# Relu and row sums: partition 4g+i reads row block g+32i, and the first row's sums are stored as 128 words

## The chip, the core and the metric

The kernel runs on one core of a Trainium2 chip. The metric is device time in microseconds (us), the median over several runs. The profiled execution is one run with the hardware profiler on. Engines named here: ACT (ScalarE), DVE (VectorE), SP (SyncE, which only issues DMAs in this kernel) and 16 DMA engines, which serve SP's one queue of transfers.

## The reference

```python
batch, seq, dim = 32, 512, 1024
x = np.random.randn(batch, seq, dim).astype(np.float32)

def reference(x):
    relu_x = np.maximum(x, 0)
    return np.sum(relu_x, axis=-1).astype(np.float32)
```

There are 16384 rows of 1024 float32 numbers (4 KB each, 67.1 MB together). Each row gives one number: the sum of its positive elements.

## The kernel before

**Rows and partitions.** SBUF has 128 partitions, so each partition gets 128 rows. The rows of DRAM are cut in three regions one after another, `REGIONS = [1, 111, 16]`: the first 128 x 1 rows, the next 128 x 111, the last 128 x 16. Within a region partition p takes block p, a contiguous piece of 1, 111 or 16 rows (lines 45 to 48, `xv`). `ov` (line 49) is the same cut of the output. `res` holds a partition's 128 sums, one column for each of its rows.

**Loads.** `buf` has three slots (`NB = 3`) of 16 rows each. Seven chunks of 16 rows (`CHUNKS`) go through the slots in turn; the first chunk is one row of the region of 1 and 15 rows of the region of 111, in two DMAs. These first two issues are moved ahead of the drain in the program's preamble (line 96), so that they are the first thing that SP does. Line 91 issues the chunks. From the fourth on, SP waits first until DVE has finished with the slot (`s_dve`, line 87). Lines 101, 112 and 115 issue the tail, the region of 16 rows: pieces of 8, 4 and 2 rows (`TAIL`), then two rows cut in four parts, the last of which lands in a tile of its own, `seam`. Behind these, still on SP, stand three stores: the sums of the first row (L117), those of the region of 111 rows (L123), and those of the tail (L207).

**Arithmetic.** For the first six chunks ACT applies the relu in place to several rows in one instruction (L145), and DVE sums the rows (L160), in the steps that `ACT_STEPS` and `DVE_STEPS` list; a few rows are done by one instruction each that does relu and sum at once, on ACT (L127) or DVE (L130). The last chunk and the tail are done in this second way, alternating between the engines. The two last rows are put together from parts in `seam`, and the last two sums release L207.

**The first row's sums.** Column 0 of `res` holds the sums of the first 128 rows of x, one in each partition. DVE transposes `res[:, 0:32]` in blocks of 32 x 32 into `turned` once the second chunk is done (L169), so that four partitions hold 32 consecutive sums each. SP waits for that (`s_turn`) and stores them as 4 pieces of 128 bytes (L117).

Of the kernel before, what the change touches and what calls it, by code (L numbers as in the profile page):

```python
# [3 lines left out]
P = 128  # L4
D = 1024
BIG = 16
NB = 3
REGIONS = [1, 111, 16]
# [3 lines left out]
TAIL = [8, 4, 2]  # L12
CUT = 912
HEAD = 256


def bass_relu_sum_kernel(
    nc: bass.Bass,
    x: bass.AP,
    out: bass.AP,  # L20
):

    fp32 = mybir.dt.float32
    ALU = mybir.AluOpType
    AF = mybir.ActivationFunctionType
    X = mybir.AxisListType.X

    B, S, _ = x.shape
    J = B * S // P
    NBIG = len(CHUNKS)
    assert BIG * NBIG + sum(TAIL) + 2 == J == sum(REGIONS)  # L40

    xr = x.rearrange("b s d -> (b s) d")
    of = out.rearrange("b s -> (b s)")
    start = [sum(REGIONS[:i]) for i in range(len(REGIONS))]
    xv = [
        xr[P * s : P * (s + n), :].rearrange("(p j) d -> p j d", p=P)
        for s, n in zip(start, REGIONS)
    ]
    ov = [of[P * s : P * (s + n)].rearrange("(p j) -> p j", p=P) for s, n in zip(start, REGIONS)]

    buf = nc.alloc_sbuf_tensor("buf", [P, NB, BIG, D], fp32)
    w = D - CUT
    seam = nc.alloc_sbuf_tensor("seam", [P, 2 + w + HEAD + 2], fp32)
    res = nc.alloc_sbuf_tensor("res", [P, J], fp32)
    turned = nc.alloc_sbuf_tensor("turned", [P, 32], fp32)

    n_in = NBIG + len(TAIL) + 3
    s_in = [nc.alloc_semaphore(f"s_in{i}") for i in range(n_in)]
    s_act = nc.alloc_semaphore("s_act")
    s_dve = nc.alloc_semaphore("s_dve")  # L60
    s_fact = nc.alloc_semaphore("s_fact")
    s_fdve = nc.alloc_semaphore("s_fdve")
    s_half = nc.alloc_semaphore("s_half")
    s_seam = nc.alloc_semaphore("s_seam")
    s_last = nc.alloc_semaphore("s_last")
    s_turn = nc.alloc_semaphore("s_turn")
    s_store = nc.alloc_semaphore("s_store")
    s_out = nc.alloc_semaphore("s_out")

    sp, act, dve = nc.sync, nc.scalar, nc.vector  # L70

    NTWO = len(ACT_STEPS)
    done = [sum(map(len, DVE_STEPS[: c + 1])) for c in range(NTWO)]


    tb = NBIG % NB


    code = nc.main_func.blocks[0].instructions
    arrival = next(  # L80
        i
        for i, ins in enumerate(code)
        if ins.engine == mybir.EngineType.SP and type(ins).__name__ == "InstDrain"
    )
    for c in range(NBIG + 1):
        if c >= NB:
            sp.wait_ge(s_dve, done[c - NB])
        if c < NBIG:
            i = 0
            for g, j, n in CHUNKS[c]:  # L90
                sp.dma_start(  # L91
                    out=buf[:, c % NB, i : i + n, :], in_=xv[g][:, j : j + n, :]
                ).then_inc(s_in[c], 16)
                i += n
                if c == 0:
                    code.insert(arrival, code.pop())
                    arrival += 1
    r = 0
    tail = []
    for i, n in enumerate(TAIL):  # L100
        sp.dma_start(out=buf[:, tb, r : r + n, :], in_=xv[-1][:, r : r + n, :]).then_inc(  # L101
            s_in[NBIG + i], 16
        )
        tail.append((r, n, s_in[NBIG + i]))
        r += n


    rows = xv[-1].rearrange("p j d -> p (j d)")[:, r * D : (r + 2) * D]
    flat = buf[:, tb, r : r + 2, :].rearrange("p j d -> p (j d)")
    first, second, third = [(0, CUT), (D + D // 2, 2 * D), (D + HEAD, D + D // 2)]  # L110
    for k, (lo, hi) in enumerate((first, second, third)):
        sp.dma_start(out=flat[:, lo:hi], in_=rows[:, lo:hi]).then_inc(  # L112
            s_in[NBIG + len(TAIL) + k], 16
        )
    sp.dma_start(out=seam[:, 2 : 2 + w + HEAD], in_=rows[:, CUT : D + HEAD]).then_inc(s_seam, 16)
    sp.wait_ge(s_turn, 1)
    sp.dma_start(  # L117
        out=of[0:P].rearrange("(k q) -> k q", q=32), in_=turned[0:P:32, 0:32]
    ).then_inc(s_store, 16)
    sp.wait_ge(s_fact, 1)  # L120
    sp.wait_ge(s_fdve, 1)
    sp.wait_ge(s_in[-1], 16)
    sp.dma_start(out=ov[1][:, :], in_=res[:, start[1] : start[2]]).then_inc(s_store, 16)  # L123


    def on_act(t, acc):
        return act.activation(t, t, AF.Relu, accum_out=acc)  # L127

    def on_dve(t, acc):
        return dve.tensor_scalar(  # L130
            out=t, in0=t, scalar1=0.0, scalar2=None, op0=ALU.max, op1=ALU.add, accum_out=acc
        )

    def row(c, i):
        return buf[:, c % NB, i, :], res[:, c * BIG + i : c * BIG + i + 1]

    k = 0
    for c in range(NTWO):
        alone = BIG - sum(ACT_STEPS[c])
        act.wait_ge(s_in[c], 16 * len(CHUNKS[c]))  # L140
        r = 0
        ready = []
        for n in ACT_STEPS[c]:
            t = buf[:, c % NB, r : r + n, :]
            act.activation(t, t, AF.Relu).then_inc(s_act, 1)  # L145
            k += 1
            ready += [k] * n
            r += n
        for i in range(BIG - alone // 2, BIG):
            on_act(*row(c, i))  # L150
        if alone:
            dve.wait_ge(s_in[c], 16 * len(CHUNKS[c]))
            for i in range(BIG - alone, BIG - alone // 2):
                on_dve(*row(c, i))
        r = seen = 0
        for n in DVE_STEPS[c]:
            if ready[r + n - 1] > seen:
                seen = ready[r + n - 1]
                dve.wait_ge(s_act, seen)
            dve.tensor_reduce(  # L160
                out=res[:, c * BIG + r : c * BIG + r + n],
                in_=buf[:, c % NB, r : r + n, :],
                axis=X,
                op=ALU.add,
            ).then_inc(s_dve, 1)
            r += n
        if c == 1:
            dve.wait_ge(s_dve, done[c])
            dve.transpose(out=turned[:, :], in_=res[:, 0:32]).then_inc(s_turn, 1)  # L169


    j0 = NBIG * BIG
    for c in range(NTWO, NBIG):
        act.wait_ge(s_in[c], 16 * len(CHUNKS[c]))
        dve.wait_ge(s_in[c], 16 * len(CHUNKS[c]))
        for i in range(BIG):
            ins = (on_act if i % 2 else on_dve)(*row(c, i))
            if i >= BIG - 2:
                ins.then_inc(s_fact if i % 2 else s_fdve, 1)
    for r, n, s in tail:  # L180
        act.wait_ge(s, 16)
        dve.wait_ge(s, 16)
        for i in range(r, r + n):
            f = on_act if (i - r) % 2 else on_dve
            f(buf[:, tb, i, :], res[:, j0 + i : j0 + i + 1])

    lo, hi = first
    act.wait_ge(s_in[-3], 16)
    dve.wait_ge(s_in[-3], 16)
    on_act(flat[:, lo : CUT // 2], seam[:, 0:1]).then_inc(s_half, 1)  # L190
    on_dve(flat[:, CUT // 2 : hi], seam[:, 1:2]).then_inc(s_half, 1)
    k = 2 + w
    lo, hi = second
    act.wait_ge(s_in[-2], 16)
    on_act(flat[:, lo:hi], seam[:, k + HEAD : k + HEAD + 1]).then_inc(s_seam, 1)
    lo, hi = third
    dve.wait_ge(s_in[-1], 16)
    on_dve(flat[:, lo:hi], seam[:, k + HEAD + 1 : k + HEAD + 2]).then_inc(s_seam, 1)
    act.wait_ge(s_seam, 16 + 2)
    act.wait_ge(s_half, 2)  # L200
    on_act(seam[:, 0:k], res[:, J - 2 : J - 1]).then_inc(s_last, 1)
    dve.wait_ge(s_seam, 16 + 2)
    on_dve(seam[:, k : k + HEAD + 2], res[:, J - 1 : J]).then_inc(s_last, 1)


    sp.wait_ge(s_last, 2)
    sp.dma_start(out=ov[-1][:, :], in_=res[:, start[-1] : J]).then_inc(s_out, 16)  # L207
    sp.wait_ge(s_store, 16 * (len(REGIONS) - 1))
    sp.wait_ge(s_out, 16)


# [26 lines left out]
```

## Time and profile before

| | |
|---|---|
| median of 3 runs | 160.86 us (160.80 to 160.87) |
| span of the profiled execution | 159.4 us |
| what lies around the span (160.86 less 159.39) | 1.47 us |
| DVE busy | 120.6 us, 59 instructions |
| ACT busy | 101.5 us, 54 instructions |
| DMA packets | 2457, 67.18 MB, 421 GB/s over the span |

The profiled execution has no time of its own beside its span, which runs from the first to the last instruction of the program; the median of the runs stands for the whole. Times in views are in us from the start of the span. Besides the views of the profile, three records of the trace are used: the time and size of each DMA packet, the start and length of each DMA issue on SP, and the times at which the 16 engines add to a DMA's semaphore. Their figures for the kernel before:

| bytes of a packet | count | shortest ns | mean ns | longest ns |
|---|---|---|---|---|
| 4096 (first row) | 128 | 159 | 198 | 620 |
| 61440 (15 rows) | 128 | 2267 | 2289 | 2547 |
| 65536 (16 rows) | 768 | 2418 | 2421 | 2513 |
| 32768 (tail, 8 rows) | 128 | 1213 | 1213 | 1213 |
| 444 (L123's store) | 128 | 22 | 24 | 29 |
| 128 (L117's store) | 4 | 13 | 13 | 13 |
| 64 (L207's store) | 128 | 8 | 10 | 11 |
| 4 (semaphore writes) | 276 | 7 | 9 | 14 |

### The profile page before, as it was taken

To read this page: it belongs to the slowest core of one execution; us is meant where nothing else is said; L and a number is where in the kernel's file an instruction comes from. 1 tells how busy PE (TensorE), PEld (TensorE's weight loads), DVE (VectorE), ACT (ScalarE), POOL (GpSimd) and SP (SyncE) were. 2 spreads that over 40 slices of the span, in tenths; PEclk is the share of its full clock that TensorE was granted. 3 is DMA by queue.
4 is the path that set the end of the run, shared out by engine and by line. 5 is a ranking of instruction groups with operands and counts; after the bars stand their busy time and mean duration, and the time that the engine had idled before them with its cause. 6 is when DMAs were issued, how large, how long until landed. Compare 5 with 4: busy or idle time off the path is not lost.

```text
span 159.4 us, 150 instructions
## 1 busy us (share of the span) xinstructions
DVE 120.6 (76%) x59; ACT 101.5 (64%) x54; POOL 0.2 (0%) x4
## 2 busy tenths in 40 slices
DVE  0000000009999999999999999999999999898995
ACT  3000059980799708996099941999329980496975
POOL 0000000000000000000000000000000000000000
DMA  9997996996996997989979969969969979798994
GB/s 378 493 401 339 493 526 263 526 526 263 526 493 296 526 444 345 526 378 411 526 312 477 526 263 526 526 263 526 526 263 526 444 345 526 321 469 374 417 400 142
DMA packets 2457, 67.18 MB, mean 421 GB/s; under 512 B 536, under 2 KB 792, under 8 KB 1176
## 3 DMA queue, kind: packets, MB, share of 16 engines
q1 hardware_dynamic: 2456, 67.18, 98.1%
q14 instruction: 1, 0.01, 0.0%
HBM read 67.11 MB, written 0.07 MB: 421 GB/s over the span
## 4 chain that ended last, share of the span: by engine, by line
DVE 55%; DMA 34%; ACT 9%; SPq 2%; issue 0%
DVE res L160 54%; DMA buf<-in_x_dram 34%; ACT buf L145 9%; SPq L101 1%; SPq L112 1%; DVE buf L130 0%; DVE seam L130 0%; SPq L91 0%; DVE turned L169 0%
## 5 line engine op out<-in xcount | busy, mean ns | idle before, releaser
L160 DVE TENSOR_REDUCE res<-buf 128x4 f32<-128x4096 f32 (+3 forms) x18 | 99.4, 5596 | 35.5 <-ACT buf L145 35.5
L145 ACT ACTIVATE buf<-buf 128x7168 f32<-128x7168 f32 (+5 forms) x13 | 80.4, 6233 | 46.1 <-DMA buf<-in_x_dram 46.1
L127 ACT ACTIVATE buf<-buf 128x1024 f32<-128x1024 f32 (+2 forms) x19 | 19.0, 999 | 8.9 <-DMA buf<-in_x_dram 8.9
L130 DVE TENSOR_SCALAR_CACHE_REDUCE buf<-buf 128x1024 f32<-128x1024 f32 (+2 forms) x19 | 20.7, 1143 | 1.7 <-DMA buf<-in_x_dram 1.6
L127 ACT ACTIVATION_READ_ACCUMULATOR buf<-buf 128x1 f32 x19 | 3.6, 188 | 0.0
L145 ACT ACT_TABLE_LOAD x1 | 1.3, 1283 | 1.3 <-PEq L223 1.3
L130 DVE DVE_READ_ACCUMULATOR buf<-buf 128x1 f32 x19 | 1.6, 84 | 0.0
L130 DVE TENSOR_SCALAR_CACHE_REDUCE seam<-seam 128x258 f32<-128x258 f32 x1 | 0.4, 421 | 0.0
L127 ACT ACTIVATE seam<-seam 128x114 f32<-128x114 f32 x1 | 0.3, 300 | 0.1
L169 DVE STREAM_TRANSPOSE turned<-res 128x32 f32<-128x32 f32 x1 | 0.2, 211 | 0.0
L127 ACT ACTIVATION_READ_ACCUMULATOR seam<-seam 128x1 f32 x1 | 0.2, 186 | 0.0
L223 POOL MEMSET const-bfloat16-1.0<- 128x1 bf16 x1 | 0.1, 101 | 0.0
L223 POOL MEMSET const-uint8-127<- 128x1 uint8 x1 | 0.1, 101 | 0.0
L223 POOL MEMSET const-float32-0.0<- 128x1 f32 x1 | 0.1, 98 | 0.2 <-issue 0.2
L223 POOL MEMSET const-float32-1.0<- 128x1 f32 x1 | 0.1, 98 | 0.0
L130 DVE DVE_READ_ACCUMULATOR seam<-seam 128x1 f32 x1 | 0.1, 82 | 0.0
## 6 DMA issues: line engine op xcount, KB each, us to landing
buf<-in_x_dram SPq DMA_DIRECT2D x1, 7680.0 KB, 21.1
buf<-in_x_dram SPq DMA_DIRECT2D x1, 4096.0 KB, 25.3
buf<-in_x_dram SPq DMA_DIRECT2D x1, 2048.0 KB, 29.9
buf<-in_x_dram SPq DMA_DIRECT2D x1, 1024.0 KB, 31.9
buf<-in_x_dram SPq DMA_DIRECT2D x1, 512.0 KB, 3.3
buf<-in_x_dram SPq DMA_DIRECT2D x1, 456.0 KB, 32.5
buf<-in_x_dram SPq DMA_DIRECT2D x1, 256.0 KB, 32.7
seam<-in_x_dram SPq DMA_DIRECT2D x1, 184.0 KB, 32.6
```

The lines of the kernel that those rows point to most:

```text
L101: sp.dma_start(out=buf[:, tb, r : r + n, :], in_=xv[-1][:, r : r + n, :]).then_inc(s_in[NBIG + i], 16)
L112: sp.dma_start(out=flat[:, lo:hi], in_=rows[:, lo:hi]).then_inc(s_in[NBIG + len(TAIL) + k], 16)
L127: return act.activation(t, t, AF.Relu, accum_out=acc)
L130: return dve.tensor_scalar(out=t, in0=t, scalar1=0.0, scalar2=None, op0=ALU.max, op1=ALU.add, accum_out=acc)
L145: act.activation(t, t, AF.Relu).then_inc(s_act, 1)
L160: dve.tensor_reduce(out=res[:, c * BIG + r : c * BIG + r + n], in_=buf[:, c % NB, r : r + n, :], axis=X, op=ALU.add,).then_inc(s_dve, 1)
L169: dve.transpose(out=turned[:, :], in_=res[:, 0:32]).then_inc(s_turn, 1)
L223: nc = _bacc.Bacc("TRN2", target_bir_lowering=False, num_devices=1)
```

## The change

In each region partition 4g+i (g from 0 to 31, i from 0 to 3) takes block g+32i in the place of block 4g+i. The pieces stay contiguous and of the same size. On the DRAM side the access pattern of each load and store becomes one of 32 x 4 pieces; on the SBUF side it stays one of 128 partitions. The first row's sums are stored from column 0 of `res` directly, as 128 words of 4 bytes, once the first chunk is summed; the transpose, `turned` and `s_turn` go. `last` is 0 and `j0` is 112, so the pieces of the tail and the columns of `res` stay as they were.

```diff
--- before.py
+++ after.py
@@ -43,16 +43,18 @@
     of = out.rearrange("b s -> (b s)")
     start = [sum(REGIONS[:i]) for i in range(len(REGIONS))]
     xv = [
-        xr[P * s : P * (s + n), :].rearrange("(p j) d -> p j d", p=P)
+        xr[P * s : P * (s + n), :].rearrange("(i g j) d -> g i (j d)", i=4, g=P // 4)
         for s, n in zip(start, REGIONS)
     ]
-    ov = [of[P * s : P * (s + n)].rearrange("(p j) -> p j", p=P) for s, n in zip(start, REGIONS)]
+    ov = [
+        of[P * s : P * (s + n)].rearrange("(i g j) -> g i j", i=4, g=P // 4)
+        for s, n in zip(start, REGIONS)
+    ]
 
     buf = nc.alloc_sbuf_tensor("buf", [P, NB, BIG, D], fp32)
     w = D - CUT
     seam = nc.alloc_sbuf_tensor("seam", [P, 2 + w + HEAD + 2], fp32)
     res = nc.alloc_sbuf_tensor("res", [P, J], fp32)
-    turned = nc.alloc_sbuf_tensor("turned", [P, 32], fp32)
 
     n_in = NBIG + len(TAIL) + 3
     s_in = [nc.alloc_semaphore(f"s_in{i}") for i in range(n_in)]
@@ -63,7 +65,6 @@
     s_half = nc.alloc_semaphore("s_half")
     s_seam = nc.alloc_semaphore("s_seam")
     s_last = nc.alloc_semaphore("s_last")
-    s_turn = nc.alloc_semaphore("s_turn")
     s_store = nc.alloc_semaphore("s_store")
     s_out = nc.alloc_semaphore("s_out")
 
@@ -74,6 +75,7 @@
 
 
     tb = NBIG % NB
+    j0 = NBIG * BIG
 
 
     code = nc.main_func.blocks[0].instructions
@@ -89,38 +91,39 @@
             i = 0
             for g, j, n in CHUNKS[c]:
                 sp.dma_start(
-                    out=buf[:, c % NB, i : i + n, :], in_=xv[g][:, j : j + n, :]
+                    out=buf[:, c % NB, i : i + n, :].rearrange("p j d -> p (j d)"),
+                    in_=xv[g][:, :, j * D : (j + n) * D],
                 ).then_inc(s_in[c], 16)
                 i += n
                 if c == 0:
                     code.insert(arrival, code.pop())
                     arrival += 1
+    last = REGIONS[-1] - sum(TAIL) - 2
     r = 0
     tail = []
     for i, n in enumerate(TAIL):
-        sp.dma_start(out=buf[:, tb, r : r + n, :], in_=xv[-1][:, r : r + n, :]).then_inc(
-            s_in[NBIG + i], 16
-        )
+        sp.dma_start(
+            out=buf[:, tb, r : r + n, :].rearrange("p j d -> p (j d)"),
+            in_=xv[-1][:, :, (last + r) * D : (last + r + n) * D],
+        ).then_inc(s_in[NBIG + i], 16)
         tail.append((r, n, s_in[NBIG + i]))
         r += n
 
 
-    rows = xv[-1].rearrange("p j d -> p (j d)")[:, r * D : (r + 2) * D]
+    rows = xv[-1][:, :, (last + r) * D : (last + r + 2) * D]
     flat = buf[:, tb, r : r + 2, :].rearrange("p j d -> p (j d)")
     first, second, third = [(0, CUT), (D + D // 2, 2 * D), (D + HEAD, D + D // 2)]
     for k, (lo, hi) in enumerate((first, second, third)):
-        sp.dma_start(out=flat[:, lo:hi], in_=rows[:, lo:hi]).then_inc(
+        sp.dma_start(out=flat[:, lo:hi], in_=rows[:, :, lo:hi]).then_inc(
             s_in[NBIG + len(TAIL) + k], 16
         )
-    sp.dma_start(out=seam[:, 2 : 2 + w + HEAD], in_=rows[:, CUT : D + HEAD]).then_inc(s_seam, 16)
-    sp.wait_ge(s_turn, 1)
-    sp.dma_start(
-        out=of[0:P].rearrange("(k q) -> k q", q=32), in_=turned[0:P:32, 0:32]
-    ).then_inc(s_store, 16)
+    sp.dma_start(out=seam[:, 2 : 2 + w + HEAD], in_=rows[:, :, CUT : D + HEAD]).then_inc(s_seam, 16)
+    sp.wait_ge(s_dve, done[0])
+    sp.dma_start(out=ov[0][:, :, :], in_=res[:, 0:1], allow_slow_non_contiguous=True).then_inc(s_store, 16)
     sp.wait_ge(s_fact, 1)
     sp.wait_ge(s_fdve, 1)
     sp.wait_ge(s_in[-1], 16)
-    sp.dma_start(out=ov[1][:, :], in_=res[:, start[1] : start[2]]).then_inc(s_store, 16)
+    sp.dma_start(out=ov[1][:, :, 0 : j0 - 1], in_=res[:, 1:j0]).then_inc(s_store, 16)
 
 
     def on_act(t, acc):
@@ -164,12 +167,8 @@
                 op=ALU.add,
             ).then_inc(s_dve, 1)
             r += n
-        if c == 1:
-            dve.wait_ge(s_dve, done[c])
-            dve.transpose(out=turned[:, :], in_=res[:, 0:32]).then_inc(s_turn, 1)
-
-
-    j0 = NBIG * BIG
+
+
     for c in range(NTWO, NBIG):
         act.wait_ge(s_in[c], 16 * len(CHUNKS[c]))
         dve.wait_ge(s_in[c], 16 * len(CHUNKS[c]))
@@ -204,8 +203,8 @@
 
 
     sp.wait_ge(s_last, 2)
-    sp.dma_start(out=ov[-1][:, :], in_=res[:, start[-1] : J]).then_inc(s_out, 16)
-    sp.wait_ge(s_store, 16 * (len(REGIONS) - 1))
+    sp.dma_start(out=ov[-1][:, :, last:], in_=res[:, j0:J]).then_inc(s_out, 16)
+    sp.wait_ge(s_store, 16 * 2)
     sp.wait_ge(s_out, 16)
```

## The prediction

> **What bounds the kernel now.** I read the page's DMA rows first, because a kernel that reads 67 MB and does little arithmetic is probably bound there.
>
> ```profile
> DMA  9997996996996997989979969969969979798994
> q1 hardware_dynamic: 2456, 67.18, 98.1%
> ```
>
> Packets take 98.1% of what 16 DMA engines have in the span. The sixes among the nines are an artefact: a long packet is booked whole in the slice where it starts. The windows view, in stages, settles that (columns: busy time of DVE, ACT, POOL, clock, DMA share, GB/s):
>
> ```profile
> 21.00:80.00 59.00, 44.47 (x9) 42.09 (x6) 0.00 (x0) 1.00 1.01 435
> 80.00:137.00 57.00, 57.00 (x15) 40.37 (x12) 0.00 (x0) 1.00 0.98 425
> 137.00:157.00 20.00, 18.30 (x33) 17.03 (x33) 0.00 (x0) 1.00 0.98 413
> ```
>
> DVE too is full from 80 to 137, and the chain of waits goes through it for 54% of the span. So the second question is whether DVE ever lets the DMA queue run dry. SP's own waits say how early it reissues:
>
> ```profile
> SPq L91 <- DVE res L160: 101.6, 4, 50.7
> SPq L122 <- DMA buf<-in_x_dram: 31.0, 1, 31.0
> SPq L101 <- DVE res L160: 16.9, 1, 16.9
> SPq L207 <- DVE seam L130: 0.5, 1, 0.5
> ```
>
> SP waits for a buffer, but the last such wait ends at 122.07 (the timeline below), while the chunk still in flight finishes landing at 137.7 (its 16 semaphore events). A refill is queued some 15 us before it is needed. Hence DMA is the bound from its first packet (1.01 us, packet records) to the last load landing (157.44), and DVE only follows. The chain of work has the ends:
>
> ```profile
> 0.00 0.39 SPq L91
> ...
> 0.45 21.14 DMA buf<-in_x_dram
> ...
> 124.39 32.60 DMA buf<-in_x_dram
> ...
> 157.01 0.44 DVE buf L130 x2
> 157.45 0.02 issue
> 157.47 0.43 DVE seam L130 x2
> ```
>
> So three stretches set the time: SP's first issue up to the first packet, the transfer, and the end (last sums, then L207's store). The change touches all three through DMA alone. The issue times on SP are therefore the next view:
>
> ```profile
> 0.00 0.86 SPq L91 DMA_DIRECT2D buf<-in_x_dram  x2
> ...
> 124.87 0.44 SPq L115 DMA_DIRECT2D seam<-in_x_dram  x1
> 125.35 0.63 SPq L117 DMA_DIRECT2D out_dram<-turned  x1
> ...
> 157.08 0.34 SPq L123 DMA_DIRECT2D out_dram<-res  x1
> 157.93 0.34 SPq L207 DMA_DIRECT2D out_dram<-res  x1
> ```
>
> Every DMA with 128 rows issues in 0.33 to 0.34 us alone, 0.39 as the first, 0.42 to 0.50 behind another. The only one of another form, L117 (4 rows of 32 words), takes 0.63, although it makes 4 packets and not 128. What decides is the form of the pattern, not the packets.
>
> **The changed loads: issue.** After the change the DRAM side of every load and store counts 32 x 4 rows and no longer 128, while the SBUF side still counts 128. No row has that pair. Bounds: 0.34 (the form does not matter) and 0.63 (L117, the only form that differs). I take 0.63, since L117 is the one row whose pattern is not a plain 128. Could it be dearer, with one more dimension than L117? I allow 0.2 us more per end for the range, the distance between the two forms once again, as an estimate.
>
> Where does that count? L91's first issue: 0.63 - 0.39 = 0.24 us. Nothing covers it; the first packet moves from 1.01 to about 1.25, and the whole transfer with it. The second issue of L91 is covered by the 4 KB packets before it, 8 per engine at 159 ns or more (1.3 us). The first two issues also stand ahead of the start barrier, for whose end ACT waits 1.3 us before its table load; that moves by about 0.4, under 19.1 us of ACT's wait for the first chunk. L91's later issues and L101, L112, L115 (seven by 0.19, so 1.3 us) lie under the 15 us of queued transfer; without that cover they would cost those 1.3 us. L123 begins at 157.08 and would end 0.29 later, at 157.71, still ahead of L207's 157.93, so that it costs nothing; the cover is 0.5 us, and an issue of over 0.85 would begin to show. L207 itself is bare: 0.63 - 0.34 = 0.29 us, and the first packet, 0.83 us after its issue began, moves with it. Sum: +0.24 + 0.29 = +0.53 us, with bounds 0 and +0.93.
>
> **The changed loads: addresses.** Same bytes, same packet sizes (each partition's piece stays contiguous in DRAM), in another order over DRAM. What is to be gained is the excess of packets over the shortest of their size, per engine. 4 KB: 8 x (198 - 159) = 0.31 us. 60 KB: 8 x (2289 - 2267) = 0.18. 64 KB: 48 x (2421 - 2418) = 0.16. The tail's: 0.13. Sum 0.78 us. Of the 0.31, 0.20 belongs to each engine's first packet (up to 620 ns), which is a start and no matter of order. So 0.55 us at most can go, and the 64 KB packets stand within 0.2% of their shortest: the middle has nothing to give. A loss is bounded by the slowest records: 48 x (2513 - 2421) = +4.4 us if every 64 KB packet were as slow as the slowest. I take -0.1 us (a little of the early excess, where 16 engines start in step), as the records lie almost all at their shortest. Ends: -0.55 and +4.4.
>
> A rule speaks against the change here. The tail's blocks are of 16 rows, so after the change partitions 4g and 4g+1 lie 32 x 64 KiB = 2 MiB apart. The row: before, blocks lie 64 KiB apart there, a power of two as well, and 32 KB packets take 1213 ns in all 128 records, 27.0 GB/s per engine, as fast as the 64 KB packets of the 111-row blocks (27.1). Powers of two as such do no harm at this rate. The Trainium skill ("DMA: Bandwidth & Descriptors", section Latency and other measured facts) says that row pitches of large powers of two slow copies, 164 GB/s at 2 MiB against 214 with padding; by that ratio, an estimate, the tail's 8.39 MB would take 25.2 us for 19.3, and the time would be 5.9 us longer. No run here shows a pitch of 2 MiB.
>
> **The first row's store.** Gone are a transpose on DVE (0.21 us at 70.11, and the wait before it) and L117's wait on it. DVE has the queue's 15 us behind it, so this gains nothing; without that cover it would be 0.2 us. The store becomes 128 packets of 4 bytes, 8 per engine, in the place of 4 of 128 bytes. Words of 4 bytes take 9 ns in the records of semaphore writes, 64 bytes 10, 128 bytes 13: 8 x 13 = 0.1 us per engine at most. They stand in the queue behind the seam's load and ahead of L123's store, whose packets begin at 157.93, and the engines are idle from 157 on. Landed they must be only when L209's wait ends at 159.35. Even one after another, 128 x 13 ns = 1.7 us from 157.24 end at 158.9. So I take 0. L117 itself keeps its place on SP at 125.35, after which SP waits 31 us for L122; its cost there is covered.
>
> The Trainium skill (the same page, section Specifications) says that below 512 bytes the DMA engine reads, modifies and writes. Taken as twice the packet time, an estimate, that is 0.2 us per engine and changes nothing in the sum.
>
> **The sum.** The profiled span is 159.39 us, the median of runs 160.86, so 1.47 us lie around the span and stay. 160.86 + 0.53 - 0.10 = 161.29, say 161.3: slower by 0.27%. About 0.2%, which is 0.32 us, is what can be told from no change; so this forecast stands just beyond it.
>
> **The rivals.**
> 1. *The issue form does not matter* (0.34 stays). For: L117 is odd also in that it runs on 4 rows, so its 0.63 may come from that alone, not from the pattern. Against: it does a 32nd of the packets and should then be cheaper. Time: 160.86 - 0.1 = 160.8, no change.
> 2. *The new order takes away the early excess and the issue stays cheap:* 160.86 - 0.55 = 160.3, faster. This is the only way to a gain that I can work out, since the middle is at its shortest packet; it needs both.
> 3. *The new order collides in DRAM.* The 64 KB packets, now 2418, lengthen; from 2425 on (48 x 7 ns = 0.3 us) it shows, and at the slowest record it is 160.86 + 0.53 + 4.4 = 165.8. For: the engines' packets move in step early, and 212 and 280 ns of excess are seen before 8 us. Against: it dies out at once, with no excess over 99 ns later.
> 4. *The words' store becomes the last wait:* it decides only if 128 words take over 2.1 us from 157.24, 16 ns each one after another; at 30 ns each, +1.7 us.
>
> **How the numbers follow.** Forecast 0.60 (161.0 to 161.8: its own range, from -0.4 of relief to +0.93 of issue); rival 1 with the same issue but a little loss or gain, 0.17; rival 2 0.08; rival 3 0.09; rival 4 0.03; anything else 0.03. Of the forecast's 0.60 some 0.10 lie under 161.18 and count as no change; rivals 3 and 4 count as slower, and of rival 2 and the rest a part each as faster. Faster 0.10, same 0.26, slower 0.64. The range 160.5 to 162.2 leaves out most of rivals 2 and 3.
>
> **What would show it.** Right: the first issue on SP and the last store's at 0.6 us, the first packet near 1.25, the last load landing near 157.6, 64 KB packets still at 2418, the span near 159.8. Wrong: issues still at 0.34 (rival 1), packets of 64 KB over 2425 (rival 3), or a last wait that ends on the words' store (rival 4).

## The result, and the profile after

The changed kernel takes 165.66 us in the median of 4 runs (165.48 to 166.48), the kernel before 160.85: a ratio of 1.0307, interval 1.0283 to 1.0330. The change costs 4.8 us. The forecast was 161.3 us with a range of 160.5 to 162.2: it had the kernel slower, as it is, but by 0.4 us.

First the page and the windows of the changed kernel (columns of the windows: stretch, length, busy time of DVE, ACT and POOL, clock, DMA share, GB/s):

```profile
span 163.6 us, 149 instructions
DMA  9979996999899799699699799899979969989950
q1 hardware_dynamic: 2592, 67.18, 95.7%
```

```profile
21.00:80.00 59.00, 43.69 (x8) 41.75 (x5) 0.00 (x0) 1.00 1.03 443
80.00:137.00 57.00, 57.00 (x15) 40.70 (x12) 0.00 (x0) 1.00 0.98 424
137.00:157.00 20.00, 18.39 (x32) 16.16 (x31) 0.00 (x0) 1.00 0.97 411
157.00:163.60 6.60, 1.36 (x6) 1.66 (x6) 0.00 (x0) 1.00 0.13 35
```

The middle runs at the rate of before (435, 425 and 413 GB/s there). The last digit of the DMA row, 0, and the last window say where the time went: after 157 there are 6.6 us in which almost no bytes move, against 2.4 in the kernel before:

```profile
157.00:159.40 2.40, 0.86 (x4) 0.76 (x4) 0.00 (x0) 1.00 0.13 31
```

SP's waits name what is waited for there:

```profile
SPq L125 <- DMA buf<-in_x_dram: 30.2, 1, 30.2
SPq L105 <- DVE res L163: 16.7, 1, 16.7
SPq L208 <- DMA out_dram<-res: 4.1, 1, 4.1
SPq L206 <- DVE seam L133: 0.3, 1, 0.3
```

L208 is the final wait for the stores: 4.1 us. In the kernel before it was L209's:

```profile
SPq L209 <- DMA out_dram<-res: 1.1, 1, 1.1
```

The timeline of SP has the rest:

```profile
0.00 1.29 SPq L93 DMA_DIRECT2D buf<-in_x_dram  x2
...
126.46 0.60 SPq L120 DMA_DIRECT2D seam<-in_x_dram  x1
127.11 0.61 SPq L122 DMA_DIRECT2D out_dram<-res  x1
157.97 0.57 SPq L126 DMA_DIRECT2D out_dram<-res  x1
158.84 0.54 SPq L206 DMA_DIRECT2D out_dram<-res  x1
```

Every issue is now of the long kind. One by one the issues take 0.54 to 0.66 us, and the fourth load's 0.90; in the kernel before they took 0.33 to 0.50, and L117's 0.63. A DMA engine reports that its part of a DMA has landed by adding to the DMA's semaphore; such an addition is called a post here. Cut into stretches with the records of packets and posts, the span of 163.56 us for 159.39 divides so:

| stretch | before | after | more |
|---|---|---|---|
| start to the first packet | 1.01 | 1.44 | 0.43 |
| first packet to the last load landed | 156.43 | 156.92 | 0.49 |
| to the issue of the last store | 0.49 | 0.48 | 0 |
| last store's issue to the end of its last packet | 1.04 | 1.40 | 0.36 |
| last packet's end to the store's last post | 0.38 | 3.28 | 2.90 |

These are 4.2 us. The rest lies around the span: each run's time less its own span is 1.7 to 1.9 us, where it is 1.3 to 1.4 in the runs of the kernel before (the 1.47 further up sets the median of the runs against the span of another execution). The words' 16 posts and those of L126's store share a semaphore; the 32 come in from 157.96 to 163.34, a few at a time, although all packets of both were through by 159.54. In the kernel before, the posts of the first two stores end at 159.05.

### The profile page after: what moved, and what is told of

Read it like the earlier page. It is cut to its first block, busy times and chain, and to the rows that moved or that the text cites. A ratio compares the mean times of both kernels' runs of the same rounds, so it can differ in the third digit from the quotient of the medians.

```text
span 163.6 us, 149 instructions
## 1 busy us (share of the span) xinstructions
DVE 120.4 (74%) x58; ACT 101.6 (62%) x54; POOL 0.2 (0%) x4
## 4 chain that ended last, share of the span: by engine, by line
DVE 53%; DMA 33%; ACT 8%; SPq 2%; issue 0%
DVE res L163 53%; DMA buf<-in_x_dram 33%; ACT buf L148 8%; SPq L105 1%; SPq L117 1%; SPq L93 0%; DVE buf L133 0%; DVE seam L133 0%
```

## The experiments

Two theories stood against each other for the 2.9 us. A: the 128 words take long to be written, and the later stores' semaphores stand behind them. B: the stores of 444 and 64 bytes are slow in the new order of their pieces.

**The words earlier.** The words' store is issued after the fourth chunk's load.

```diff
+        if c == NB:
+            sp.dma_start(out=ov[0][:, :, :], in_=res[:, 0:1], ...).then_inc(s_store, 16)
...
-    sp.wait_ge(s_dve, done[0])
-    sp.dma_start(out=ov[0][:, :, :], in_=res[:, 0:1], ...).then_inc(s_store, 16)
```

> The changed kernel with one edit: the store of the 128 words is issued right after the fourth chunk's load, near 54 us, and no longer behind the tail's loads. Theory A (the 128 words take long to be written, and the later stores' semaphores stand behind them): what is left late is only the start, the transfer and the longer last issue, so 165.7 - 2.9 = 162.8 us, and the last store lands some 0.4 us after its last packet where the changed kernel needed 3.3. Theory B (the stores of 444 and of 64 bytes are slow in the new order, because neighbouring pieces now come from different engines): 165.6 us, the landing stays 3 us late. In either case the trace shows how long the words alone take to land.

Measured: 166.84 us, ratio 1.0392 (1.0361 to 1.0424), more than the change itself. Neither theory's time came, but SP's last wait is short again:

```profile
SPq L208 <- DMA out_dram<-res: 1.3, 1, 1.3
```

So the late landing belongs to the words and B falls: the other two stores are in the new order here and land 0.40 to 0.43 us after their last packet. Theory A's time, 162.8 us, was missed because the cost moved with the words. The windows where the words are written (packets from 79.3 us on, posts 79.90 to 84.05):

```profile
70.00:80.00 10.00, 10.00 (x3) 5.32 (x1) 0.00 (x0) 1.00 1.10 433
80.00:90.00 10.00, 10.00 (x3) 9.27 (x2) 0.00 (x0) 1.00 0.79 229
90.00:100.00 10.00, 10.00 (x2) 4.68 (x1) 0.00 (x0) 1.00 1.06 459
```

The kernel before, in the same window:

```profile
80.00:90.00 10.00, 10.00 (x3) 10.00 (x2) 0.00 (x0) 1.00 0.97 419
```

229 GB/s for 419. 27 packets of 64 KB that start behind the words, from 79.45 to 86 us, take 3.0 to 6.7 us each, where some 2.42 is usual. So the loads queued behind the words are held up while these are written and some 5 us longer (the last of the 27 ends at 89.1); how, the records do not say. Neither of the two places that were tried is cheap: at the end the words lengthen the last wait, in the middle they slow the loads.

**The words alone.** The kernel before, with this store in the old order and no transpose.

```diff
-    sp.wait_ge(s_turn, 1)
-    sp.dma_start(
-        out=of[0:P].rearrange("(k q) -> k q", q=32), in_=turned[0:P:32, 0:32]
-    ).then_inc(s_store, 16)
+    sp.wait_ge(s_dve, done[0])
+    sp.dma_start(out=ov[0][:, :], in_=res[:, 0:1], ...).then_inc(s_store, 16)
...
-        if c == 1:
-            dve.wait_ge(s_dve, done[c])
-            dve.transpose(out=turned[:, :], in_=res[:, 0:32]).then_inc(s_turn, 1)
```

> The kernel before with only the first row's store changed: 128 words from column 0 in the old order (partition p to word p), no transpose; all loads and the other stores as before. Theory A: 160.9 + 2.9 = 163.8 us, the last store landing some 3 us late. Theory A2 (only words that different engines interleave are slow): less, 160.9 to 162. Theory B: 160.9 us, no change.

Measured: 165.98 us, ratio 1.0328 (1.0311 to 1.0344), more than the 163.8 of theory A. With the old order and the short issues everywhere, the words in place of the transpose cost as much as the whole change, so A2's forecast of less falls: the old order of the words is no better.

```profile
SPq L202 <- DMA out_dram<-res: 5.7, 1, 5.7
```

**All the rest.** The changed kernel without the words' store.

```diff
-    sp.dma_start(out=ov[0][:, :, :], in_=res[:, 0:1], ...).then_inc(s_store, 16)
...
-    sp.wait_ge(s_store, 16 * 2)
+    sp.wait_ge(s_store, 16)
```

> The changed kernel without the first row's store (those 128 sums are not written). It prices all the rest of the change. The sum of the prediction for this rest: 161.3 us. Rival (as in the kernel before with long issues, where some engines got the second load's packets 1 to 1.5 us late): 161.4 to 163.5, about 162.7 in the median, the slowest engine's first 60 KB packet starting after 4 us.

Measured: 162.58 us (162.52 to 163.73), ratio 1.0121 (1.0099 to 1.0143). Words alone +5.1, rest alone +1.7, both +4.8: they do not add. Part of it is counted twice, since the 0.4 to 0.5 us around the span that come with the missing transpose (below) are in both. For the rest, the words begin when the first engines are through with their loads, near 156.7 us with the words alone and 157.3 in the changed kernel, and their stretch ends at 163.8 and 163.3; by these times what else is late in the changed kernel runs under it.

**Why words are slow.** Here the words stored one by one are a column that lies 444 bytes apart:

```diff
-    sp.dma_start(out=ov[0][:, :, :], in_=res[:, 0:1], ...)
+    sp.dma_start(out=ov[1][:, :, 0:1], in_=res[:, 1:2], ...)
...
-    sp.dma_start(out=ov[1][:, :, 0 : j0 - 1], in_=res[:, 1:j0])
+    sp.dma_start(out=ov[1][:, :, 1 : j0 - 1], in_=res[:, 2:j0])
```

> The changed kernel, but the 128 words that are stored one by one are column 1 of the sums, which belong 444 bytes apart in DRAM, and not column 0, whose words lie side by side in 512 bytes; the sums of the first row are not stored, and the store of the long region writes 440 bytes a piece. Theory A3 (words are slow because 128 of them from 16 engines fall into the same 512 bytes, one after another at some 50 ns): the words land in under 1 us and the time falls to that of the kernel without them, 161.3 to 163. Theory A4 (a word of 4 bytes costs some 50 ns wherever it goes): no change, 165.7 us.

Measured: 163.01 us, ratio 1.0124 (1.0105 to 1.0142), beside 162.58 without words. A3 holds: the same number of words of the same size costs little or nothing when they lie apart. The profiled execution's span is 0.57 us longer than that without words, and its transfer 0.62 longer: that is a late engine at the start (table further down), not the words. SP's last wait:

```profile
SPq L208 <- DMA out_dram<-res: 1.3, 1, 1.3
```

Then the number and the spread of the words, in the kernel with the words alone (comments give each run's operands):

```diff
+    # 64 side by side:  out=ov[0][0:64, :],  in_=res[0:64, 0:1]
+    # 16 side by side:  out=ov[0][0:16, :],  in_=res[0:16, 0:1]
+    # 64, every other:  out=ov[0][0:P:2, :], in_=res[0:P:2, 0:1]
```

> The kernel before with the words' store in the old order, as in the run that took 166.0 us, but for partitions 0 to 63 alone: 64 words (the other 64 sums of the first row are not stored). Theory A (one word after another, some 50 ns each): the words land 3.2 us sooner, near 160.6 us in the span, and the time is 162.4 to 162.8 us. Rival (a fixed wait that a store of words has, whatever their number): 166 us.

> The kernel before with the words' store in the old order, but for partitions 0 to 15 alone: 16 words side by side in 64 bytes (the other 112 sums of the first row are not stored). 128 words took some 6.4 us to land and 64 took 7, so it is not the number of words. Theory E (words in the same 64 bytes go one after another, some 0.4 us each, different 64 bytes at the same time; 128 and 64 words both have 16 in each): again 16 in a row, 6.4 us, landing near 163.6 us, 165.7 us. Rival E2 (the piece is 256 bytes: 64 words at 0.1 us): 1.6 us, landing near 158.9, 161.3 us. Rival E3 (a fixed wait of any store of words side by side): 165.7 us as well, which the next run tells apart.

> The same, for every other partition: 64 words, 8 bytes apart, over all 512 bytes (the other 64 sums of the first row are not stored). Theory E: 8 words in each 64 bytes, 3.2 us, landing near 160.5 us, 162.6 us; 64 words side by side took 165.7. Rival E3 (a fixed wait): 165.7 us.

The final wait of SP in the three, in this order:

```profile
SPq L202 <- DMA out_dram<-res: 6.1, 1, 6.1
```

```profile
SPq L202 <- DMA out_dram<-res: 1.4, 1, 1.4
```

```profile
SPq L202 <- DMA out_dram<-res: 2.4, 1, 2.4
```

| words | span of addresses | words in 256 bytes | time, us | ratio (interval) | last word packet to last post on the words' semaphore, us |
|---|---|---|---|---|---|
| 128 | 512 bytes | 64 | 165.98 | 1.0328 (1.0311 to 1.0344) | 6.7 |
| 64 side by side | 256 | 64 | 165.68 | 1.0309 (1.0293 to 1.0326) | 7.2 |
| 64, every other | 512 | 32 | 162.83 | 1.0123 (1.0109 to 1.0136) | 3.5 |
| 16 side by side | 64 | 16 | 161.55 | 1.0039 (1.0024 to 1.0053) | 2.5 |

Half the words side by side cost as much as all, half the words spread over twice the bytes cost half. That excludes one price per word wherever it goes, and a fixed wait. The expectation of theory E, pieces of 64 bytes, fell with the 16 words, which it had at 165.7. Pieces of 128 bytes would make the 16 words as dear as the 64 on every other place, and pieces of 512 the 64 side by side half as dear as the 128; neither came. So, if the output begins where a piece does, the time goes by the number of words in the same 256 bytes, and different pieces of 256 bytes go on at the same time, as rival E2 has it: some 0.1 us a word for 32 and 64 words.

The 16 words are another matter. The last column counts to the posts of the store queued behind the words, which end at 159.05 even in the kernel before, so that 2.5 is only an upper bound. The first 16 posts on the semaphore are the words' own, since they come before that store's first packet (157.94): they end at 157.63, 0.6 us after the last word's packet. That is 0.04 us a word, where E2 had 0.1 and 1.6 us. So 0.1 us is no constant price, and whether the words of a piece really go one after another stays open. In the run of 16 each DMA engine has one word, in the others four or eight; no run separates the number of words in a piece from the number that one engine has there. What the memory does in this time no run shows.

**The issue.** The kernel before, in its order, with every DMA kept off the short issue by a switch of the library:

```diff
+    nc.dge_precook = False
```

> The kernel before with one line added that keeps every DMA off the short issue, in the old order. Theory of the issue form (the +0.43 us of the first packet and the +0.36 us from the last store's issue to its last packet both come from the longer issue alone): 160.85 + 0.8 = 161.65 us, first packet at 1.44 us. Rival (the issue itself gives +0.27 and +0.20, the rest is the new order): 161.3 us, first packet near 1.28.

Measured: 162.70 us, from 161.36 to 163.51 run by run; ratio 1.0103 (1.0066 to 1.0139). The first packet comes at 1.415, near the changed kernel's 1.437, and from the last store's issue to its last packet it is 1.34 us (1.40 there): the issue's form explains nearly all of both ends, the new order is not needed for them. But the rest of this time, 1 us over the expected 161.65, lies in neither end. Two runs went after it, and then a third:

```diff
     # new order in the region of 111 rows only (its loads and its store)
-    in_=xv[g][:, j : j + n, :]
+    in_=mid[:, :, j * D : (j + n) * D]        # "(i g j) d -> g i (j d)"
```

> The kernel before with the new order in the region of 111 rows alone, its loads and its store; the first row and the tail are as before. Theory C (the transfer's +0.49 us is the new order in the long blocks): 160.85 + 0.5 = 161.35 us. Rival C2 (it came from the start: the first row's new order or the later first issue put the engines apart): 160.9 us, 64 KB packets still at 2421 ns in the mean. Theory B for the 444-byte store: its landing and the last store's come up to 2.9 us late, 163.8 us; theory A: no late landing.

```diff
     # old order, long issue in the same region only
+    nc.dge_precook = g != 1
```

> The kernel before, in the old order, with the long issue on the loads and the store of the region of 111 rows alone: the same DMAs have the long issue as in the run with the new order in the middle region, which took 163.5 us. Theory D (that time came from the long issue of the second load, for which some engines wait at the start): 163 to 163.5 us, two or more engines starting their 60 KB packets after 3.5 us. Theory C (it came from the new order in DRAM): 160.9 to 161.2 us, all 60 KB packets started by 3 us.

```diff
     # old order, long issue on all loads but the first two
+    nc.dge_precook = c == 0
```

> The kernel before, in the old order, with the long issue on all loads from the second chunk on and on the tail's; the first two loads and all stores keep the short one. Theory D2 (the late engines at the start come from the long issue of the second load): 160.85 us, as before, in every run. Rival D3 (they come from the third and fourth load's long issues, 1.7 to 3 us into the span, while the second load's first packets go out): 160.9 to 163.3 us, changing from run to run.

The new order in the middle: 163.48 us (162.84 to 163.87), ratio 1.0158 (1.0138 to 1.0177). None of the times expected for it came but B's, and that by another path: its last store lands 0.44 us after its last packet, while its transfer is 2.0 us longer (table). The long issue there in the old order: 162.19 in the median of 9 runs (160.82 to 163.30), where theory D had 163 to 163.5 and theory C at most 161.2. Long issues from the third load on: 160.89 (160.74 to 160.96), 1.0001 (0.9993 to 1.0010), with these in its timeline of SP:

```profile
122.14 1.76 SPq L102 DMA_DIRECT2D buf<-in_x_dram  x3
123.94 1.90 SPq L113 DMA_DIRECT2D buf<-in_x_dram  x3
125.89 0.61 SPq L116 DMA_DIRECT2D seam<-in_x_dram  x1
```

So long issues in the middle and in the tail are covered, and D3 falls. What is left is the second load's, alone or together with those behind it; no run has that one alone. The profiled executions show how:

| kernel | first packet | start of the last engine's first 60 KB packet | first 60 KB packets over 2700 ns | first packet to last load landed |
|---|---|---|---|---|
| before | 1.01 | 2.94 | 0 | 156.43 |
| long from the third load on | 1.04 | 2.98 | 0 | 156.57 |
| changed | 1.44 | 3.37 | 1 | 156.92 |
| changed, without words | 1.45 | 3.32 | 4 | 156.82 |
| the same, transpose kept | 1.45 | 3.29 | 0 | 156.45 |
| changed, words apart | 1.45 | 3.68 | 2 | 157.44 |
| long middle, old order | 1.03 | 3.17 | 4 | 157.22 |
| new order in the middle | 1.02 | 4.04 | 2 | 158.39 |
| long everywhere, old order | 1.42 | 4.62 | 4 | 158.48 |

With a long second issue some engines start late or have a first long packet of 2.7 to 3.4 us in place of 2.3. The lag stays: with the new order in the middle, the 16 posts of a load lie 2.4 us apart at 41 us and still 2.1 us apart at the end. It happens in the old order as well, and not in every run. Why some engines get it and others not stays open, and so does whether the new order adds to it: with long issues on the same DMAs it took 163.48 us in the median and the old order 162.19, but the second issue was longer too (0.65 us for 0.57).

**The transpose.** The changed kernel without words, with the transpose on DVE put back, which nobody reads:

```diff
+        if c == 1:
+            dve.wait_ge(s_dve, done[c])
+            dve.transpose(out=turned[:, :], in_=res[:, 0:32]).then_inc(s_turn, 1)
```

> The changed kernel without the first row's store, as in the run that took 162.58 us, but with the transpose on DVE kept (nobody reads it; the first row's sums are not stored). What lies around the span was 1.36 us in all kernels that have the transpose and 1.7 to 2.0 in all that do not. Theory F (that 0.5 us comes with taking out the transpose, not with the stores): 162.1 us, 1.36 around the span. Rival: 162.6 us, 1.85 around the span.

Measured: 163.04 us (162.68 to 164.50), ratio 1.0147 (1.0119 to 1.0174): the 1.31 to 1.41 us around the span are back (1.80 to 1.97 without the transpose), as theory F has it, but its 162.1 us did not come. The last wait is longer than the 1.3 us of the run without the transpose:

```profile
SPq L212 <- DMA out_dram<-res: 2.6, 1, 2.6
```

In the trace a packet of 8 KB on the instruction queue runs from 159.70 to 160.57, within the last store's packets (159.62 on). The last 8 of these follow only from 160.57 on, and one engine's store lands at 161.56, the other fifteen by 160.19. In the kernels without the transpose the instruction packets, two in number, come after the span. In the kernel before the one such packet starts at 159.21, after the store's last packet. That the fetch delayed that one engine, and that its place sets what lies around the span, is inferred from the times.

## Why the prediction was wrong

**The step that failed is the first row's store, taken at 0.** I priced a word by its packet (9 to 13 ns), and even "one after another" by that: 1.7 us. But a packet's record can end long before the write does: with the words alone, the last word's packet ends at 157.05 and the last post on their semaphore comes at 163.77. In the changed kernel the words, two pieces of 256 bytes with 64 words each, take from 157.3 to 163.34 us to land. The prediction's own rival 4 had the wait and the threshold (over 16 ns each from 157.24), though not the cause; with the measured 48 ns a word (6.1 us by 128) its rule gives +4.0 us of span, and 4.2 was measured. It got a chance of 0.03, because I took packet times for the cost of a write. That the two differ stood in the trace of before: L117's 4 packets were through at 156.63, and its posts came at 157.15 to 157.32. How much it would be for words, no row there showed.

The Trainium skill ("DMA: Bandwidth & Descriptors", section Specifications) says that below 512 bytes the engine reads, modifies and writes. The runs show that the size alone is not what costs: words 444 bytes apart and pieces of 64 bytes land quickly. Of what was run here only 32 and more words in the same 256 bytes are slow, and by far more than the factor of two that I estimated from the page.

**The issue** was right in kind. L117's 0.63 us was the row to price by: the long issues take 0.54 to 0.66, the fourth load's up to 1.6 (words apart). Its sum was a little small, +0.53 against 0.43 + 0.36 = 0.79 us, within the bound of 0.93: the packets come later after the issue's end as well, 0.78 us for 0.62 at the start and 0.65 for 0.50 at the end. The cover of the later issues held (ratio 1.0001). The cover that I claimed for the second load, the 4 KB packets before it, did not: with a long second issue the transfer takes 0 to 2.0 us more, changing from run to run.

**The addresses** were right to about 0.1 us. In the run with the transpose kept, all in the new order, the transfer took 156.45 us for 156.43 before, and 64 KB packets 2421 ns in the mean, as before; so rival 3 falls. The changed kernel's own profile has 2426 there, just over the 2425 that I set as the sign of rival 3, but that sign was too fine: the old order with long issues from the third load on has 2424.6, and takes no longer than the kernel before (ratio 1.0001). The ceiling for the gain was added up a little low, 0.55 us where its own terms give 0.78 - 0.20 = 0.58, and the tail's loads have 0.08 us of excess and not 0.13; the forecast does not hang on either.

The Trainium skill's row on HBM row pitches (same page, Latency and other measured facts) is on copies between HBM tensors with all 128 rows at one pitch. Here only runs of four partitions lie 2 MiB apart, and the data go to SBUF. The loss that I estimated from it did not come: the tail's 32 KB packets still take 1213 ns, and the measurement decides for this case.

**The transpose** gained nothing, as I said, but without it 0.4 to 0.5 us more lie around the span, where the sum had what lies around it stay.

The kernel without words shows what the sum would have been worth: 162.58 against my 161.3. Of the 1.3 us between, 0.3 are the issue, 0.5 lie around the span, and the other 0.5 are late engines at the start with the 0.1 of relief that did not come.

None of the versions run here beats the kernel before. Its transpose, which puts 32 sums side by side so that the first row leaves in 4 pieces of 128 bytes, is what keeps the words away.

## What to carry to other kernels

A write is not over when its packet is: look at the posts. Do not let dozens of single words from several partitions fall into the same 256 bytes, least of all in a queue with other work behind it; gather them in SBUF first, as the transpose does here. Two late stretches that end at the same wait do not add, so price each by when it starts. And where an access pattern changes form, look at the issue time of the first and second load and of the last store, which had no cover here.

## What the runs showed of the hardware that was not expected

- Words of 4 bytes into the same 256 bytes: 32 land in 3.5 us, 64 in 6.7 to 7.2, some 0.1 us each, but 16 within 0.6; two pieces of 256 bytes go on at the same time (128 words in 512 bytes: 6.7).
- Words that are not yet written hold up the loads queued behind them: 64 KB packets of up to 6706 ns in place of some 2420, 229 GB/s in place of 419 over 10 us.
- A DMA whose DRAM side counts 32 x 4 and whose SBUF side 128 issues in 0.54 to 0.66 us as a rule, a plain 128 to 128 in 0.33 to 0.50, and its packets start 0.15 us later after the issue's end.
- With long issues from the second load on, some engines can be 1 us or more behind for the whole kernel (first packet to last load landed 157.22 to 158.48 us for 156.43); with long issues from the third load on none was (156.57).
- In every run without the transpose the instruction fetch at the end comes after the span and not within it, and 0.4 to 0.5 us more lie outside the span (1.6 to 2.0 us for 1.3 to 1.4).
